# Modulation weights laid out transposed, their columns summed on VectorE

## The chip, the core and the metric

The kernel runs on one core of a Trainium2 chip. The metric is the device time of one execution in microseconds; the time before is the median of three runs. The engines are named as in the profile: PE is TensorE (matmuls and transposes) with PEld its weight loads, DVE is VectorE, ACT is ScalarE, POOL is GpSimd, SP is the queue from which all DMAs are issued. A transpose is a matmul with the identity.

## The reference, cut to what matters

A trunk of two layers works on 256 tokens of 1024 features, in float32. Each layer has three sub-layers, and each sub-layer is a norm with a modulation that depends on one conditioning vector `c`:

```python
cond = jax.nn.silu(c)
for layer in range(DEPTH):
    mod = cond @ mod_w[layer] + mod_b[layer]          # (1, 9 * 1024)
    sh1, sc1, g1, sh2, sc2, g2, sh3, sc3, g3 = jnp.split(mod, 9, axis=-1)
    h = rms_norm(x, norm_g[layer, 0]) * (1 + sc1) + sh1
    x = x + 0.5 * g1 * swiglu(h, w_gate, w_up, w_down)
    ...                                               # attention or convolution, then a second SwiGLU
return rms_norm(x, final_norm_g)
```

A SwiGLU has 2816 hidden columns. The mixer of layer 0 is a gated spatial product and an attention side by side, that of layer 1 a short convolution. `mod_w` is (2, 1024, 9216), so 18 vectors of 1024 values are each a product of `cond` with a 1024 x 1024 block of weights (4 MB); it is a matrix times a vector.

## The kernel before, in words

The residual stream is kept transposed, features on the 128 partitions and tokens along the free axis (`xT`, eight chunks of 128 features). Each float32 operand of a product is split into a part of 12 bits (`h_...`, a copy on ACT, `split_hi`) and a rest (`l_...`, a subtraction on DVE, `split_lo`), and a product is three float32r matmuls (`mm3`, line 140 in the profile, since all matmuls are recorded in the helper `mm`). Weights come in units of 1 MB by `load` (line 300) into four raw buffers (`w_g`, `w_u`, `w_d` and so on); each half of a unit is split, and a raw buffer is free when both rests are made. Helpers record all operations, so line 177 is every two-operand DVE operation, 188 every DVE operation with a scalar and a tensor, 183 every one with scalars alone, 204, 209 and 214 the activations, copies and scalings on ACT, 223 the masks on POOL.

Every engine works in the order in which the program emits. A planner (`Pace`, `clk`) keeps estimated times for each engine; `pump` and `fill_dve` issue the splits of coming weights and the steps of the modulation where they fit before the products issued so far end.

The modulation beyond the first two vectors: `mod_load` (line 390, `mw`) brings 256 rows of one block, 1 MB, rows of 4 KB. `mod_step` multiplies 128 rows x 512 columns by the matching part of `cond` (one value for each partition) and adds it to an accumulator `acc` on DVE; 16 such steps make a vector. `mod_flush` then sums over the partitions: four transposes on PE into `pm`, a row sum on DVE (`red`), and `mod_column` adds bias and gain. `mod_need` forces all of a vector before its use. There are 16 such vectors.

The start (lines 1214 to 1415) is written out by hand. `c` is transposed, `cond` made; the squares of x are summed by row, x over its rms is transposed for the norm (`pxn`) and x itself for the residual (`px`); small vectors come in five loads as rows and are transposed. Then, for each of eight chunks of 128 features (`dc`): the shift and scale columns of the chunk (`start_mod`, line 1230, `mws`, four DMAs of 256 KB with rows of 512 B) are accumulated in eight steps (`start_steps`, two on ACT and six on DVE), summed over the partitions by eight matmuls with a column of ones (`start_sum`, `pm_start`), and finished by two small DVE operations; `start_h` makes the modulated chunk `t1s` and its part `hh` on ACT, DVE the rest `hl`; then 36 products with the chunk's rows of the first three pairs of hidden columns (units `s`, 384 KB for gate and up each, rows of 3 KB) are added in the banks `ps`. After the eighth chunk the other columns of the first SwiGLU follow (`pf`), two of them ahead of the rows of its second product (`pd`). The mixer's sub-layer begins with `peh`, its scores are `z`, its spatial weights are loaded at line 870 as `ws_in` and transposed in `turn_ws` into `wsT`. The tiles `wsT`, `vb`, `qT` and `kT` serve as spare weight halves through the first SwiGLU.

Of the kernel before, what the change touches and what calls it, by code (L numbers as in the profile page):

```python
# [93 lines left out]
def trunk(ctx: ExitStack, tc: tile.TileContext, x, c, mod_w, mod_b, norm_g,  # L94
          ffn_w_gate, ffn_w_up, ffn_w_down, hy_w_in, hy_w_out, gm_vnorm_g,
          gm_w_s, gm_b_s, sc_w_in, sc_conv_w, sc_w_out, final_norm_g, out):
# [131 lines left out]
    rows_c = const.tile([8, P], F32, name="rows_c")  # L228
    nc.sync.dma_start(out=rows_c, in_=c.rearrange("b (r p) -> (b r) p", p=P))
    x_in = new(rawp, "raw", "x_in", RAW, (P, 2048)).rearrange("p (t d) -> p t d", t=2)  # L230
    for t in range(2):
        nc.sync.dma_start(out=x_in[:, t, :], in_=x[0, t * P:(t + 1) * P, :])
        clk.put(x_in[:, t, :], 6000.0 + 1600 * t)
    clk.put(rows_c, 3700.0)
    clk.dma = 5700.0
# [16 lines left out]
    # columns: norm_g (2 x 3 x 8) | final_norm_g (8) | conv_w (3 x 8) | vnorm_g (4)  # L252
    rows_a = const.tile([84, P], F32, name="rows_a")
    rows_b = const.tile([72, 2, P], F32, name="rows_b")
    cols_a = const.tile([P, 84], F32, name="cols_a")
    cols_b = const.tile([P, 2, 72], F32, name="cols_b")
    cond = const.tile([P, NC], F32, name="cond")
    G0, FG, CW, VG = 0, 48, 56, 80

    def load_rows(more):  # L260
        if not more:
            nc.sync.dma_start(out=rows_a[0:48, :], in_=norm_g.rearrange("l s (r p) -> (l s r) p", p=P))
            nc.sync.dma_start(out=rows_b, in_=mod_b.rearrange("l (r p) -> r l p", p=P))
        else:
            nc.sync.dma_start(out=rows_a[48:56, :], in_=final_norm_g.rearrange("(r p) -> r p", p=P))
            nc.sync.dma_start(out=rows_a[56:80, :], in_=sc_conv_w.rearrange("o w (r p) -> (o w r) p", p=P))
            nc.sync.dma_start(out=rows_a[80:84, :], in_=gm_vnorm_g.rearrange("o (r p) -> (o r) p", p=P))

# [116 lines left out]
    def mod_load():
        i = mq["load"]
        l, v = mod_units[i // 4]
        part = i % 4
        raw = new(mrawp, "mraw", f"mw{l}{v}{part}", MRAW, (P, 2048))
        nc.sync.dma_start(out=raw.rearrange("p (k n) -> p k n", k=2),  # L390
                          in_=mod_w[l, part * 256:(part + 1) * 256, v * D:(v + 1) * D].rearrange(
                              "(k p) n -> p k n", p=P))
# [8 lines left out]
    def can_mod():  # L401
        return mq["units"] < len(mod_units) and mq["step"] // 4 < len(mod_loaded) and \
            (mq["step"] % 16 or len(mod_pending) < 3)

    def mod_step():
        """a row chunk of the weights times its part of cond, added to one of the two halves"""
        n = mq["step"]
        l, v = mod_units[mq["units"]]
        raw, t = mod_loaded[n // 4]
        kc, h = n % 16 // 2, n % 2  # L410
        if kc == 0:
            mq["acc", h] = new(accp, "acc", f"acc{l}{v}{h}", 4, (P, 512))
# [11 lines left out]
        if kc == 7:
            mod_pending.append((l, v, h, acc, clk.dve))
            if h == 1:
                mq["units"] += 1

    def mod_column(l, v, h, src, dst):
        """adds the bias; scales become a = g * (1 + scale), the halved residual its 0.5"""  # L430
        one = slice(4 * h, 4 * h + 4)
        if v % 3 == 1:
            stt(dst, src, 1.0, mod_g(l, v)[:, one], ALU.mult, ALU.mult)
            tt(dst, dst, bias_c[:, l, v * 8 + 4 * h:v * 8 + 4 * h + 4], ALU.add)
        else:
            half = v % 3 == 2 and v // 3 != 1
            stt(dst, src, 0.5 if half else 1.0, bias_c[:, l, v * 8 + 4 * h:v * 8 + 4 * h + 4], ALU.mult, ALU.add)
# [5 lines left out]
    def mod_flush(force=False):  # L443
        """sums one unit over the partitions"""
        if not mod_pending or (mod_pending[0][4] + 200 > clk.pe and not force):
            return
        l, v, h, acc, t = mod_pending.pop(0)
# [3 lines left out]
        if (l, v) not in mod_cols:  # L451
            mod_cols[(l, v)] = const.tile([P, NC], F32, name=f"mod{l}{v}")
        dst = mod_cols[(l, v)][:, 4 * h:4 * h + 4]
        red = new(accp, "red", f"red{l}{v}{h}", 3, (P, 4))

        def finish():
            sum_v(red, pm.rearrange("p (j n) -> p j n", j=4))
            mod_column(l, v, h, red, dst)
# [1030 lines left out]
```

## Time and profile before

| | before |
|---|---|
| median of three runs | 1007.77 us (1007.18 to 1008.58) |
| span of the profiled execution | 1006.8 us |
| PE busy | 995.6 us (99%), 8176 matmuls |
| DVE busy | 790.6 us (79%), 1230 instructions |
| ACT busy | 502.9 us (50%) |
| POOL busy | 16.7 us (2%) |
| HBM read | 247.32 MB, 247 GB/s over the span |
| chain that ended last | PE 95%; SPq 2%; DMA 2% |

The chain that ended last is followed back from the last instruction, at each step to what released it. Busy time of PE overlaps between neighbouring matmuls, which are pipelined. "DMA share" is the mean busy share of the core's 16 DMA engines; it can come out a little above 1. [...]

### The profile page before, as it was taken

The page shows a single profiled execution, that of the slowest core. Times are in us where ns is not written, and L with a number is a line of the kernel's source. Part 1 is how long each engine was busy: PE and PEld are TensorE (multiplying, and loading weights), DVE is VectorE, ACT ScalarE, POOL GpSimd, SP SyncE. Part 2 cuts the span into 40 slices and gives each one's busy share as a digit, 9 for nine tenths or more (in the row PEclk, how much of TensorE's full clock was granted, in tenths as well). Part 3 has the DMA queues.
Part 4 walks back from the last instruction along what each step waited for, and adds up shares of the span by engine and source line. Part 5 has one row for each costly group of instructions (what it writes and reads, how often), then busy time and mean ns, then how long its engine had stood idle before and what let it go on. Part 6 is the DMA issues. An engine that isn't in the chain of part 4 may idle for free.

```text
span 1006.8 us, 19541 instructions
## 1 busy us (share of the span) xinstructions
PE 995.6 (99%) x8176; PEld 981.4 (97%) x8176; DVE 790.6 (79%) x1230; ACT 502.9 (50%) x716; POOL 16.7 (2%) x28
## 2 busy tenths in 40 slices
PE   7999999999999999999999999999999999999998
PEld 7899999999789999999999999999999999999998
DVE  6788978889878998878789888878899797444532
ACT  6575434355756754343367434335644465434333
POOL 0000000000320000000000000000000000000000
PEclk9999999999999999999999999999999999999999
DMA  9998987965866499887964988798359538555401
GB/s 281 323 371 296 355 318 277 328 216 177 331 236 205 132 309 358 299 313 279 323 208 157 346 302 324 273 329 280 125 171 327 172 102 281 205 194 183 168 2 42
DMA packets 159857, 249.63 MB, mean 248 GB/s; under 512 B 4525, under 2 KB 125337, under 8 KB 159769
## 3 DMA queue, kind: packets, MB, share of 16 engines
q1 hardware_dynamic: 159768, 248.39, 71.8%
q8 instruction: 64, 1.05, 0.4%
q14 instruction: 25, 0.20, 0.1%
HBM read 247.32 MB, written 1.05 MB: 247 GB/s over the span
## 4 chain that ended last, share of the span: by engine, by line
PE 95%; SPq 2%; DMA 2%; DVE 0%; ACT 0%; issue 0%; ACTq 0%
PE pf L140 43%; PE pd L140 25%; PE pe L140 3%; PE pc L140 3%; PE pdh L140 2%; PE pcb L140 2%; PE pdc L140 2%; PE ps L140 2%; PE pm L144 1%; SPq L1230 1%; PE z L140 1%; PE pu L140 1%; PE pvb L140 1%; PE peh L140 1%; PE pec L140 1%; PE pv L140 1%
## 5 line engine op out<-in xcount | busy, mean ns | idle before, releaser
L140 PE MATMUL pd<-ah,h_d 128*128 128x256 f32 x704 | 200.0, 284 | 0.0
L140 PE MATMUL pd<-ah,l_d 128*128 128x256 f32 x704 | 198.3, 282 | 0.0
L140 PE MATMUL pd<-al,h_d 128*128 128x256 f32 x704 | 197.8, 281 | 0.0
L140 PE MATMUL pf<-hh,h_u 128*128 128x256 f32 x608 | 171.8, 283 | 0.0
L140 PE MATMUL pf<-hh,l_g 128*128 128x256 f32 x608 | 171.1, 281 | 0.0
L140 PE MATMUL pf<-hh,h_g 128*128 128x256 f32 x608 | 171.0, 281 | 0.0
L140 PE MATMUL pf<-hl,h_g 128*128 128x256 f32 x608 | 171.0, 281 | 0.0
L140 PE MATMUL pf<-hl,h_u 128*128 128x256 f32 x608 | 170.9, 281 | 0.0
L140 PE MATMUL pf<-hh,l_u 128*128 128x256 f32 x608 | 170.8, 281 | 0.0
L188 DVE SCALAR_TENSOR_TENSOR acc<-mw,cond,acc 128x512 f32<-128x512 f32 x224 | 158.3, 750 | 3.1 <-DMA mw<-in_mod_w_dram 3.1
L209 ACT CAST h_d<-w_d 128x1024 fp32r<-128x1024 f32 x88 | 88.4, 1047 | 127.1 <-PE pf L140 102.5
L177 DVE TENSOR_TENSOR l_d<-w_d,h_d 128x1024 fp32r<-128x1024 f32 x88 | 104.7, 1221 | 48.2 <-ACT h_d L209 48.2
L177 DVE TENSOR_TENSOR l_g<-w_g,h_g 128x1024 fp32r<-128x1024 f32 x82 | 100.0, 1220 | 52.1 <-ACT h_g L209 52.1
L209 ACT CAST h_g<-w_g 128x1024 fp32r<-128x1024 f32 x82 | 85.8, 1047 | 108.7 <-issue 75.2
L140 PEld LDWEIGHTS pd<-al,h_d 128*128 128x128 f32 x704 | 132.7, 188 | 0.0
L140 PEld LDWEIGHTS pd<-ah,h_d 128*128 128x128 f32 x704 | 132.5, 188 | 0.0
L140 PEld LDWEIGHTS pd<-ah,l_d 128*128 128x128 f32 x704 | 132.5, 188 | 0.0
L209 ACT CAST h_u<-w_u 128x1024 fp32r<-128x1024 f32 x82 | 85.9, 1047 | 65.2 <-PE pd L140 51.2
L140 PEld LDWEIGHTS pf<-hl,h_u 128*128 128x128 f32 x608 | 114.9, 189 | 0.0
L140 PEld LDWEIGHTS pf<-hh,l_u 128*128 128x128 f32 x608 | 114.8, 189 | 0.0
L140 PEld LDWEIGHTS pf<-hh,l_g 128*128 128x128 f32 x608 | 114.8, 189 | 0.0
L140 PEld LDWEIGHTS pf<-hh,h_u 128*128 128x128 f32 x608 | 114.7, 189 | 0.0
(324 smaller groups left out, 2041.2 us busy)
## 6 DMA issues: line engine op xcount, KB each, us to landing
mw<-in_mod_w_dram SPq DMA_DIRECT2D x64, 1024.0 KB, 8.2
w_d<-in_ffn_w_down_dram SPq DMA_DIRECT2D x44, 1024.0 KB, 7.1
w_g<-in_ffn_w_gate_dram SPq DMA_DIRECT2D x41, 1024.0 KB, 7.2
w_u<-in_ffn_w_up_dram SPq DMA_DIRECT2D x41, 1024.0 KB, 5.5
mws<-in_mod_w_dram SPq DMA_DIRECT2D x28, 256.0 KB, 6.2
w_ho<-in_hy_w_out_dram SPq DMA_DIRECT2D x4, 1024.0 KB, 10.9
w_cc<-in_sc_w_in_dram SPq DMA_DIRECT2D x4, 1024.0 KB, 5.2
w_cx<-in_sc_w_in_dram SPq DMA_DIRECT2D x4, 1024.0 KB, 5.2
```

What stands on the lines that cost most here:

```text
L140: return nc.tensor.matmul(out=out_, lhsT=lhsT, rhs=rhs, start=start, stop=stop, skip_group_check=True)
L144: nc.tensor.transpose(out=out_, in_=in_, identity=idn)
L177: nc.vector.tensor_tensor(out=out_, in0=a, in1=b, op=op)
L188: nc.vector.scalar_tensor_tensor(out=out_, in0=a, scalar=s, in1=b, op0=op0, op1=op1)
L209: nc.scalar.copy(out=out_, in_=in_)
L1230: nc.sync.dma_start(out=parts[i][:, :, v, :], in_=src[:, :, v, dc * P:(dc + 1) * P])
```

## The change

The arrays are handed over in other layouts. `mod_w` becomes (layer, vector, chunk, feature on the partition, 1024 inputs): a chunk of 128 outputs is one contiguous block of 512 KB. x comes transposed, the spatial weights too, and all small vectors come as one array of columns, 128 x 228. `cond` is now wanted along the free axis on all partitions: eight small matmuls with a selector spread it to 128 x 1024. One column of 128 modulation values is one DVE operation, `dot_v`: a product of 128 x 1024 weights with `cond`, times a gain, summed along the row, with the bias as first value. Accumulators, the transposes into `pm`, row sums and `mod_column` go. In the start x needs no transposes: squares, a sum by matmuls with `mean_w`, logarithm and exponential over 128 x 256 and three Newton steps give 1 / rms on all partitions; the first chunk of x over rms is made on DVE, seven on POOL (`mul_p`). The order of the eight chunks is rewritten: scale first, then shift.

```diff
-WARM = (40, 10, 0)
+WARM = (6, 14, 24)
...
-            elif can_mod() and max(clk.dve, mod_loaded[mq["step"] // 4][1]) + 660 <= t:
+            elif can_mod() and max(clk.dve, mod_ready()) + 1200 <= t:
...
+    def dot_v(src, dst, scale, init):
+        ins = [src, cond] + aps(scale, init)
+        fill_dve(ins, [dst, src])
+        nc.vector.tensor_tensor_reduce(out=src, in0=src, in1=cond, scale=scale, scalar=init, op0=ALU.mult,
+                                       op1=ALU.add, accum_out=dst)
+        return clk.op("dve", free(src) / 0.96 + 130, ins, [dst, src])
...
+    def mul_p(out_, a, b):
+        nc.gpsimd.tensor_tensor(out=out_, in0=a, in1=b, op=ALU.mult)
...
+    xT = const.tile([P, NC, S], F32, name="xT")
+    for i in range(2):
+        nc.sync.dma_start(out=xT[:, 4 * i:4 * i + 4, :], in_=x[:, 4 * i:4 * i + 4, :])
+    cols_sb = const.tile([P, 228], F32, name="cols_sb")
+    nc.sync.dma_start(out=cols_sb, in_=cols)
...
     def mod_load():
-        raw = new(mrawp, "mraw", f"mw{l}{v}{part}", MRAW, (P, 2048))
-        nc.sync.dma_start(out=raw.rearrange("p (k n) -> p k n", k=2),
-                          in_=mod_w[l, part * 256:(part + 1) * 256, v * D:(v + 1) * D].rearrange(
-                              "(k p) n -> p k n", p=P))
+        raw = new(mrawp, "mraw", f"mw{l}{v}{part}", MRAW, (P, 2, D))
+        nc.sync.dma_start(out=raw, in_=mod_w[l, v, 2 * part:2 * part + 2].rearrange("c p k -> p c k"))
...
     def mod_step():
-        if kc == 0:
-            ts(acc, src, cond[:, 0:1], None, ALU.mult)
-        else:
-            stt(acc, src, cond[:, kc:kc + 1], acc, ALU.mult, ALU.add)
+        dot_v(mod_loaded[n // 2][0][:, n % 2, :], mod_cols[(l, v)][:, chunk:chunk + 1], scale,
+              cols_b[:, l, v * 8 + chunk:v * 8 + chunk + 1])
...
-    def mod_flush(force=False):
-        pm = gbank(f"pm{l}{v}{h}")
-        for j in range(4):
-            tp(pm[:, j * P:(j + 1) * P], acc[:, j * P:(j + 1) * P], ident)
...
-            nc.sync.dma_start(out=ws_in[k], in_=gm_w_s[0, 4 * k:4 * k + 4].rearrange("h t s -> t h s"))
+        wsT = new(mix, "wsT", "wsT", 1, (P, 8, P))
+        nc.sync.dma_start(out=wsT, in_=gm_w_s)
+        keep_if(wsT, [[0, 8], [1, P]], ALU.is_ge)
...
-        def turn_ws(k):
-            for j in range(4):
-                tp(pw[:, j * P:(j + 1) * P], ws_in[k][:, j, :], ident)
...
     def start_mod(dc):
-            for v in range(2):
-                nc.sync.dma_start(out=parts[i][:, :, v, :], in_=src[:, :, v, dc * P:(dc + 1) * P])
+        for v in (1, 0):
+            nc.sync.dma_start(out=parts[v], in_=mod_w[0, v, dc])
...
+    sel = new(hip, "hi", "sel", HALF, (P, 1024), F32R).bitcast(F32)[0:8].rearrange("p (r m) -> p r m", r=8)
+    copy_v(sel, ident[0:8, 0:8].unsqueeze(2).to_broadcast([8, 8, P]))
+    for i in range(8):
+        mm(pcs[i // 4][:, i % 4 * P:(i % 4 + 1) * P], sel[:, i, :], ce, i % 4 == 0, True)
+    for k in range(2):
+        act(sqs[0][:, k], xT[:, 2 * k:2 * k + 2, :], AF.Square)
+    copy_v(cond[:, 0:512], pcs[0])
+    tt(sqs[0][:, 0], sqs[0][:, 0], sqs[0][:, 1], ALU.add)
+    for k in range(2):
+        act(sqs[1][:, k], xT[:, 4 + 2 * k:6 + 2 * k, :], AF.Square)
+    cp(cond[:, 512:D], pcs[1])
+    tt(sqs[1][:, 0], sqs[1][:, 0], sqs[1][:, 1], ALU.add)
+    for i in range(2):
+        for j in range(2):
+            mm(pr, mean_w, sqs[i][:, 0, j, :], i == j == 0, i == j == 1)
+    act(y0, pr, AF.Ln, bias=eps_t[:, 0:1])
+    act(y0, y0, AF.Exp, scale=-0.5)
+    newton(pr, y0, r0, m0, EPS)
+    for dc in range(NC):
+        o = xnT[dc // 4][:, dc % 4, :]
+        if dc < 1:
+            tt(o, xT[:, dc, :], r0, ALU.mult)
+        else:
+            mul_p(o, xT[:, dc, :], r0)
...
+    start_col(0, 1)
+    start_col(0, 0)
+    split_hi()
+    split_lo()
     for dc in range(NC):
+        t1 = start_h(dc)
+        if dc == 0:
+            split_hi()
         if dc + 3 < NC:
             mws[dc + 3] = start_mod(dc + 3)
         while can_load() and q["load"] < min(dc + 3, NC):
             load()
         tt(hl[:, dc, 0:S], t1, hh[:, dc, 0:S].bitcast(F32), ALU.subtract)
+        if dc + 1 < NC:
+            start_col(dc + 1, 1)
+        if dc == NC - 1:
+            while can_load():
+                load()
+        split_lo()
+        for i in range(2):
+            split_hi()
+        if dc + 1 < NC:
+            start_col(dc + 1, 0)
+        split_lo()
         parts = [take() for _ in range(2)]
-        for f in range(2 * NS):
-            if dc < NC - 1 and f == SUMS[dc]:
-                start_sum(dc + 1)
+        for i in range(2):
+            j, wh, wl = parts[i]
+            for f in range(2 * NS):
```

`start_col(dc, v)` is `dot_v` on the scale (`v` = 1) or shift (`v` = 0) of a chunk; `start_h` is now only the two ACT operations. The calls of `mod_flush` and `turn_ws` go.

## Rows read from the trace of the kernel before

**Rows 1.** Windows: us, busy us of each engine, granted clock, DMA share, GB/s.

```profile
215.00:345.00 130.00, 130.00 (x952) 118.63 (x951) 114.35 (x204) 83.19 (x135) 15.22 (x18) 1.00 0.62 215
64.43:996.60 932.17, 932.17 (x7698) 920.65 (x7698) 739.81 (x1104) 458.72 (x638) 15.22 (x18) 1.00 0.71 245
```

**Rows 2.** Chain of waits, end of the start: start us, us, what.

```profile
55.65 8.78 PE ps L140 x72
```

**Rows 3.** Timeline of the start: start us, us, engine, instruction [idle before].

```profile
4.68 1.06 ACT L204 ACTIVATE sqx<-x_in 128x1024 f32<-128x1024 f32 x1 [1.91 <-DMA x_in<-in_x_dram]
5.64 0.18 ACT L204 ACTIVATION_READ_ACCUMULATOR sqx<-x_in 128x1 f32 x1
...
14.70 0.40 ACT L209 CAST hh<-t1s 128x256 fp32r<-128x256 f32 x1
...
15.14 0.42 DVE L177 TENSOR_TENSOR hl<-t1s,hh 128x256 fp32r<-128x256 f32 x1 [0.30 <-ACT hh L209]
...
15.16 0.39 PE L140 MATMUL ps<-hh,h_s 128*128 128x256 f32 x1
```

**Rows 4.** Windows of the start and of a stretch after it, columns as above.

```profile
16.00:52.00 36.00, 32.36 (x244) 30.61 (x244) 28.00 (x67) 20.82 (x37) 0.00 (x0) 0.95 1.07 318
33.00:36.00 3.00, 3.00 (x14) 3.00 (x15) 2.43 (x7) 2.35 (x4) 0.00 (x0) 0.50 1.16 293
66.00:72.00 6.00, 6.00 (x53) 6.00 (x52) 4.94 (x9) 5.22 (x10) 0.00 (x0) 1.00 1.03 410
```

**Rows 5.** DMA issues: count, KB each, median us to landing.

```profile
mws<-in_mod_w_dram SPq DMA_DIRECT2D x28, 256.0 KB, 6.2
...
w_s<-in_ffn_w_gate_dram SPq DMA_DIRECT2D x8, 384.0 KB, 5.9
```

**Rows 6.** Tile `w_s`: idle time of its engine, us and times, until:

```profile
  DMA w_s<-in_ffn_w_gate_dram: 7.1, 4
```

**Rows 7.** Chain of waits, first SwiGLU's end and attention.

```profile
206.46 0.44 PE pm L144 x4
206.90 14.24 PE pd L140 x120
...
275.83 0.59 PE pm L144 x4
```

**Rows 8.** Groups on VectorE, whole span: busy us, mean ns, idle before.

```profile
L188 DVE SCALAR_TENSOR_TENSOR acc<-mw,cond,acc 128x512 f32<-128x512 f32 x224 | 158.3, 750 | 3.1 <-DMA mw<-in_mod_w_dram 3.1
L177 DVE TENSOR_TENSOR l_d<-w_d,h_d 128x1024 fp32r<-128x1024 f32 x88 | 104.7, 1221 | 48.2 <-ACT h_d L209 48.2
...
L177 DVE TENSOR_TENSOR al<-act,ah 128x512 fp32r<-128x512 f32 x44 | 30.4, 691 | 16.9 <-ACT ah L209 16.5
...
L198 DVE TENSOR_REDUCE red<-pm 128x4 f32<-128x512 f32 x32 | 21.9, 686 | 8.1 <-PE pm L144 8.1
```

**Rows 9.** Timeline of VectorE at the end of the start.

```profile
57.68 0.43 DVE L177 TENSOR_TENSOR hl<-t1s,hh 128x256 fp32r<-128x256 f32 x1 [1.11 <-ACT hh L209]
58.03 1.82 DVE L177 TENSOR_TENSOR l_s<-w_s,h_s 128x768 fp32r<-128x768 f32 x2
...
61.28 1.23 DVE L177 TENSOR_TENSOR l_u<-w_u,h_u 128x1024 fp32r<-128x1024 f32 x1
62.42 1.22 DVE L177 TENSOR_TENSOR l_g<-w_g,h_g 128x1024 fp32r<-128x1024 f32 x1
```

**Rows 10.** Groups on ScalarE, whole span.

```profile
L204 ACT ACTIVATE sq<-xT 128x512 f32<-128x512 f32 x20 | 12.7, 633 | 19.3 <-DVE xT L188 15.6 <-DVE sqacc L177 3.7
...
L204 ACT ACTIVATE y_pe<-pr_pe,eps_t 128x256 f32<-128x256 f32 x3 | 1.4, 478 | 5.7 <-PE pr_pe L140 5.7
```

**Rows 11.** Timeline of SP in the mixer.

```profile
243.16 1.12 SPq L870 DMA_DIRECT2D ws_in<-in_gm_w_s_dram  x2
```

**Rows 12.** Groups on GpSimd, whole span.

```profile
L223 POOL TENSOR_SCALAR_AFFINE_SELECT sp<-sp 128x256 f32<-128x256 f32 x8 | 6.9, 864 | 279.6 <-DVE sp L188 279.6
...
L223 POOL TENSOR_SCALAR_AFFINE_SELECT wsT<-wsT 128x512 f32<-128x512 f32 x2 | 2.7, 1350 | 0.0
```

More of the change, by code (lines that the diff above doesn't have):

```diff
@@ L229, in trunk @@
     nc.sync.dma_start(out=rows_c, in_=c.rearrange("b (r p) -> (b r) p", p=P))
[L230 to L235, printed above, removed]
+    xT = const.tile([P, NC, S], F32, name="xT")
+    for i in range(2):
+        nc.sync.dma_start(out=xT[:, 4 * i:4 * i + 4, :], in_=x[:, 4 * i:4 * i + 4, :])
+        clk.put(xT[:, 4 * i:4 * i + 4, :], 3600.0 + 1300 * i)
+    G0, FG, CW, VG, MB = 0, 48, 56, 80, 84
+    cols_sb = const.tile([P, 228], F32, name="cols_sb")
+    nc.sync.dma_start(out=cols_sb, in_=cols)
+    clk.put(cols_sb, 5500.0)
+    cols_a = cols_sb[:, 0:MB]
+    cols_b = cols_sb[:, MB:MB + 144].rearrange("p (l r) -> p l r", l=2)
+    clk.put(rows_c, 2300.0)
+    clk.dma = 5500.0
     ident = const.tile([P, P], F32, name="ident")
@@ L249, in trunk @@
     keep_if(negtri, [[-1, P]], ALU.is_ge, 1)
[L253 to L263, printed above, removed]
[L264 to L267 removed]
+    cond = const.tile([P, D], F32, name="cond")
     units = []
@@ L307, in can_load @@
         u = q["load"]
-        return u < len(units) and (u < RAW - 1 or ("x" if u == RAW - 1 else u - RAW) in raw_free)
+        return u < len(units) and (u < RAW or u - RAW in raw_free)
     slots = {}
@@ L401, in can_mod, with mod_ready @@
     def can_mod():
-        return mq["units"] < len(mod_units) and mq["step"] // 4 < len(mod_loaded) and \
-            (mq["step"] % 16 or len(mod_pending) < 3)
+        return mq["step"] // 2 < len(mod_loaded)
+    def mod_ready():
+        return mod_loaded[mq["step"] // 2][1]
     def mod_step():
         n = mq["step"]
-        l, v = mod_units[mq["units"]]
-        raw, t = mod_loaded[n // 4]
-        kc, h = n % 16 // 2, n % 2
-        if kc == 0:
-            mq["acc", h] = new(accp, "acc", f"acc{l}{v}{h}", 4, (P, 512))
-        acc, src = mq["acc", h], raw[:, (n % 4) * 512:(n % 4 + 1) * 512]
-        if kc == 0:
-            ts(acc, src, cond[:, 0:1], None, ALU.mult)
-        else:
-            stt(acc, src, cond[:, kc:kc + 1], acc, ALU.mult, ALU.add)
+        l, v = mod_units[n // 8]
+        chunk = n % 8
+        if chunk == 0:
+            mod_cols[(l, v)] = const.tile([P, NC], F32, name=f"mod{l}{v}")
+        scale = 1.0
+        if v % 3 == 1:
+            scale = mod_g(l, v)[:, chunk:chunk + 1]
+        elif v % 3 == 2 and v // 3 != 1:
+            scale = 0.5
+        dot_v(mod_loaded[n // 2][0][:, n % 2, :], mod_cols[(l, v)][:, chunk:chunk + 1], scale,
+              cols_b[:, l, v * 8 + chunk:v * 8 + chunk + 1])
         mq["step"] += 1
-        if n % 4 == 3:
-            mraw_free[n // 4] = clk.dve
-            mod_loaded[n // 4] = None
+        if n % 2 == 1:
+            mraw_free[n // 2] = clk.dve
+            mod_loaded[n // 2] = (None, 0.0)
             while can_mod_load():
                 mod_load()
[L424 to L437, printed above, removed]
     def mod_g(l, v):
@@ L441, in mod_g @@
         return cols_a[:, g:g + 8]
[L443 to L471 removed]
+    def mod_need(l, v):
+        while mq["step"] < 8 * (mod_units.index((l, v)) + 1):
+            mod_step()
     deferred = []
@@ L1259, in trunk @@
     clk.op("dve", 120.0, [ce], [ce])
-    tt(cond, pc[:, 0:8], ce, ALU.mult)
-    ss = const.tile([P, 2], F32, name="ss")
-    sy = const.tile([P, 2], F32, name="sy")
-    sr = const.tile([P, 2], F32, name="sr")
-    sqx = new(hip, "hi", "sqx", HALF, (P, 1024), F32R).bitcast(F32)
-    xn = [new(lop, "lo", f"xn{t}", HALF, (P, 1024), F32R).bitcast(F32) for t in range(2)]
-    for t in range(2):
-        act(sqx, x_in[:, t, :], AF.Square, accum_out=ss[:, t:t + 1])
-        clk.put(ss[:, t:t + 1], clk.act)
-        one = slice(t, t + 1)
-        ts(ss[:, one], ss[:, one], 1.0 / D, EPS, ALU.mult, ALU.add)
-        act(sy[:, one], ss[:, one], AF.Ln)
-        act(sy[:, one], sy[:, one], AF.Exp, scale=-0.5)
-        newton(ss[:, one], sy[:, one], sr[:, one], ss[:, one])
-        ts(xn[t], x_in[:, t, :], sr[:, one], None, ALU.mult)
@@ L1332, in trunk @@
-    accs = {}
-    def start_h(dc):
-        one = slice(dc, dc + 1)
-        stt(m_a[:, one], pm0[:, 2 * dc + 1:2 * dc + 2], cols_a[:, G0 + dc:G0 + dc + 1], cols_b[:, 0, 8 + dc:9 + dc], ALU.mult, ALU.add)
-        tt(m_sh[:, one], pm0[:, 2 * dc:2 * dc + 1], cols_b[:, 0, one], ALU.add)
-        t1 = new(work, "t1", f"t1s{dc}", 4)
-        act(t1, xnT[dc // 4][:, dc % 4, :], AF.Identity, scale=m_a[:, one], bias=m_sh[:, one])
-        cp(hh[:, dc, 0:S], t1)
-        return t1
-    start_steps(0, range(NC))
@@ L1360, in prepare, with start_col, start_h @@
             ts(bv[:, sub, 2], bv[:, sub, 2], 0.5, None, ALU.mult)
+    newton(pr, y0, r0, m0, EPS)
+    xnT = [mix.tile([P, 4, S], F32, tag=tag, name="xn" + tag) for tag in ("qT", "kT")]
     for dc in range(NC):
-        def steps(ks):
-            start_steps(dc + 1, ks)
-        def hs():
-            while q["h"] < 2 * dc + 2:
-                split_hi()
-        if dc > 1:
-            steps(range(2))
-        hs()
-        if dc == 1:
-            x_copies.pop()()
-            raw_free["x"] = clk.act
+        o = xnT[dc // 4][:, dc % 4, :]
[3 more added lines that the diff above has]
+            mul_p(o, xT[:, dc, :], r0)
+    hh = new(mix, "hh", "hh00", 1, (P, NC, XC), F32R)
+    hl = new(mix, "hl", "hl00", 1, (P, NC, XC), F32R)
+    state["h"] = (hh, hl)
+    m_sh = const.tile([P, NC], F32, name="mod00")
+    m_a = const.tile([P, NC], F32, name="mod01")
+    mod_cols[(0, 0)], mod_cols[(0, 1)] = m_sh, m_a
+    def start_col(dc, v):
+        one = slice(dc, dc + 1)
+        if v:
+            dot_v(mws[dc][1], m_a[:, one], cols_a[:, G0 + dc:G0 + dc + 1], cols_b[:, 0, 8 + dc:9 + dc])
+        else:
+            dot_v(mws[dc][0], m_sh[:, one], 1.0, cols_b[:, 0, one])
+    def start_h(dc):
+        one = slice(dc, dc + 1)
+        t1 = new(work, "t1", f"t1s{dc}", 4)
+        act(t1, xnT[dc // 4][:, dc % 4, :], AF.Identity, scale=m_a[:, one], bias=m_sh[:, one])
+        cp(hh[:, dc, 0:S], t1)
+        return t1
+    start_col(0, 1)
+    start_col(0, 0)
+    split_hi()
+    split_lo()
+    sbanks = [gbank(f"ps{f}") if f < 4 else dbank(f"ps{f}") for f in range(2 * NS)]
+    for dc in range(NC):
+        t1 = start_h(dc)
+        if dc == 0:
+            split_hi()
         if dc + 3 < NC:
```

175 lines of the change are left out of this document (38 added, 137 removed).

## The prediction

> **What bounds the kernel now.** I read the windows by stage first. From 64.43 to 996.60 us TensorE is busy 932.17 of 932.17 us at a granted clock of 1.00, while VectorE is at 739.81 and the DMA share at 0.71 [rows 1]. There a microsecond of TensorE work that disappears is a microsecond of time, and work on VectorE costs nothing until it delays an operand of a product. The start is another kernel: its products `ps` run from 15.16 to 64.43 us [rows 2, 3]. Inside it the DMA share is 1.07 and yet only 318 GB/s move, while 410 GB/s move a little later at a share of 1.03 [rows 4]; the later stretch fetches rows of 4 KB, the start mostly rows of 512 B. The casts of the weights, which stand on ScalarE in front of each chunk's `hh`, wait 7.1 us for weights [rows 6].
>
> **The change, part by part.** The sum is made against the profiled span of 1006.8 us; the median of the runs, 1007.77 us, lies 0.97 us above it, which I carry over.
>
> *Transposes of the modulation sums.* The 128 transposes of `pm` go (16 vectors, two halves, four each). On the chain of waits a group of four takes 0.44 us, a few in the attention 0.59 [rows 7]. 32 x 0.44 = 14.1 us, at most 32 x 0.59 = 18.9. They stand among products that wait for nothing, so 14.1 us go from the end. The eight transposes of the spatial weights are two groups of the same kind: 0.9 us. In the attention such groups may fill gaps of a dependent chain; eight of them stand there, some 3.5 us to 4.7, which a gap could take back. TensorE shows no idle time from 215 to 345 us [rows 1], so I count them as gained and keep their loss for the range.
>
> *VectorE, steady part.* Out go 224 updates (158.3 us) and 32 row sums (21.9) [rows 8], together 180 us, and 32 first steps and the small columns besides. In come 128 `dot_v`, each a product of two 1024-wide float32 operands with a sum beside it. The trace has no such operation. From below: the plain 1024-wide TENSOR_TENSOR, 1.22 us long and followed after 1.14 us [rows 9]. From above: two cycles for each element. The 1024-wide and the 512-wide TENSOR_TENSOR (1221 and 691 ns) differ by 0.53 us for 512 elements [rows 8], so 1024 elements more in cycles add 1.06: 2.2 us. Nearest is the plain row, plus 0.06 us for scalars read by pointer (750 against 691 ns for 512 elements), plus something for delivering the sum, where ScalarE's accumulator read shows 0.18 us [rows 3]. I take 1.28 us from one start to the next. 128 x 1.28 = 164 us against 180: VectorE gets lighter, off the path, and the time stays.
>
> *The start, head.* Out go 32 transposes of x, three of small vectors, their copies on ScalarE and 64 matmuls of column sums. In come four squares (0.63 us each), a logarithm and an exponential of 256 columns (0.48 each) [rows 10], three Newton steps on VectorE, four matmuls. x's first half is there at 4.68 us, as now [rows 3]; its second at 5.9, as half a megabyte at 0.4 MB/us takes 1.3. Squares end at 7.1, their sum on VectorE at 7.8 (0.69, as the 512-wide row), four float32 matmuls at some 8.8 (estimate), logarithm and exponential at 9.8, Newton and the first chunk of x over rms (four steps of 0.4, by `hl`) at 11.5, two dots at 14.1, then the modulated chunk on ScalarE (0.6, an addressed scale and bias) and `hh` (0.40): the first product starts at about 15.1, as now [rows 3]. Removing the transposes of x gains nothing at the head; it moves the wait from TensorE to the line of norm and dots.
>
> *The start, cadence.* Eight chunks of 128 features follow one another. TensorE needs 36 products each; 72 take 8.78 us [rows 2], so 4.4. The DMA brings 1.05 MB of modulation and 0.79 MB of weights [rows 5]: 5.8 us at the present 318 GB/s, 4.6 at 400. Each modulation row is now 4 KB instead of 512 B and each weight row stays at 3 KB, so I take 400. VectorE has `hl` 0.35, two splits 1.82 [rows 9], two dots 2.56 and some 0.25 us of waiting for `hh` behind the second dot: 4.97 us. VectorE binds. Now the eight `hl` run from 15.14 to 57.68 us [rows 3, 9], 6.08 us apart. New: 15.1 + 7 x 4.97 + 4.7 = 54.6 us for the end of `ps`, against 64.43: a gain of 9.8 us. All chunks (15.9 MB with x) have landed at 43 us by that rate; the next two loads of 1 MB wait only for buffers that VectorE's rests free, and land before 54.
>
> *Queues.* On SP 32 loads of modulation become 16, and five loads of small vectors become one ahead of them; nothing there is late. The spatial weights now go straight into `wsT`, which holds spare weight halves until the first SwiGLU's products end at 221.1 us [rows 7]; the present loads are issued at 243.16 [rows 11]. So no wait on SP, where `bs_bc` and the next weights are queued behind. The mask on GpSimd is one pass of 1024 columns for two of 512 (1.35 us each) [rows 12], earlier than now, on an idle engine; without that cover it would cost 2.7 us once. Seven products of x over rms go to GpSimd, one needed per chunk; its row with 256 columns takes 0.86 us [rows 12], so they end about 6 us after Newton and stay ahead of a chunk each 4.97.
>
> Sum: 14.1 + 0.9 + 9.8 = 24.8 us. 1006.8 - 24.8 + 0.97 = **983 us**.
>
> **Rivals.**
>
> *The dots run at half rate (slower).* Price 2.2 us each. In the start VectorE's cadence becomes 0.35 + 1.82 + 4.4 + 0.25 = 6.8 us, the first product comes at 17, `ps` ends at 17 + 7 x 6.8 + 4.7 = 69.3: 4.9 us lost. In the steady part 282 us of dots replace some 202, so VectorE stands at 820 of 917 us; and the order of issue is written by a planner whose formula counts 1.2 us a dot, so each dot keeps splits and SwiGLU products waiting a microsecond longer than planned. Of these 128 us VectorE's idle time, 192 us [rows 1], takes most; I put a fifth, 24 us, on TensorE: 1007.8 + 4.9 - 15.0 + 24 = 1022. It is slower from 11 us of such stalls upward. Against it: an update with two SBUF operands takes 750 ns for 512 elements [rows 8], the full rate. [...] Chance 0.08.
>
> *The start stays bound by the DMA, or its head is late.* If 318 GB/s are not a matter of row length, the cadence is 5.8 us and `ps` ends at 15.1 + 7 x 5.8 + 4.7 = 60.4, a gain of 4.0 instead of 9.8: **989 us**. The same time comes out if GpSimd's seven products (6 us) hold up VectorE's first dots. [...] Against: 410 GB/s in rows 4. [...] Chance 0.22, with the case that the attention takes back its 3.5 us (986).
>
> *The start gains more.* With dots at 1.14 and no wait for `hh` the DMA's 4.6 binds: 15.1 + 7 x 4.6 + 4.7 = 52.0, so 980. That is the forecast's own lower side.
>
> *The removed transposes do not show.* They are on the chain, so only if TensorE's place is taken by something not seen: 0.02.
>
> **How the numbers follow.** Forecast (980 to 986) 0.68, DMA or head (986 to 995) 0.22, half rate 0.08, nothing 0.02. The range goes from 977, where the `pm` groups in the attention count 0.59 and the head comes 2 us earlier, to 994, the second rival with the attention's loss; it leaves out the half-rate case and little else. About 0.2% (2 us) is what a measurement of this kernel can tell from no change. Faster 0.90, same 0.02, slower 0.08.
>
> **What would show it.** Right: no rows of `pm` and `pws`; a dot followed after about 1.28 us; TensorE without idle time from the end of `ps`, which lies at 54 to 55 us; eight `hl` 5.0 us apart; over 370 GB/s in the start. Wrong: dots above 2 us, TensorE idle between the end of `ps` and 790 us; or casts that wait for weights through the start at 320 GB/s.

## The result, and the profile after

The changed kernel takes 990.77 us (median of four runs, 990.55 to 990.80) against 1007.47 us (median of four, 1006.60 to 1008.58) for the kernel before in the same comparison: ratio 0.9835, 95% interval 0.9822 to 0.9848. That is faster, as forecast, and 7.8 us above the forecast of 983. The profiled execution has a span of 989.1 us and a time of its own of 990.8 us, so 1.7 us lie around the span where the prediction carried 0.97: 0.7 us of the miss. In the later runs of the kernel before, too, the time is 1.7 to 1.8 us above the span of the same run, so the execution that I had profiled, with 1006.8 us, was about 0.8 us longer than the median one. The other 7.1 us are in the trace, and one view finds them: the chain of waits at the end of the start.

```profile
56.70 0.41 ACT hh L216
...
57.13 0.44 DVE hl L176
...
57.62 4.53 PE ps L139 x35
62.14 7.98 PE pf L139 x67
```

The start ends at 62.14 us (before 64.43): 2.3 us gained where 9.8 were forecast. From there to the end are 926.96 us (before 942.4): 15.4 us gained where 15.0 were forecast. So the steady part came out as predicted, well within the 2 us by which runs of the kernel before differ, and the start misses 7.5 us.

**Steady part.** Windows of the changed kernel (us, busy us of PE, PEld, DVE, ACT, POOL, granted clock as a share of full speed, DMA share, GB/s), which answer to [rows 1]:

```profile
215.00:345.00 130.00, 129.90 (x950) 118.81 (x949) 113.04 (x198) 85.27 (x138) 13.35 (x17) 1.00 0.60 215
...
62.14:979.00 916.86, 916.76 (x7559) 905.51 (x7558) 709.72 (x1029) 457.57 (x635) 13.35 (x17) 1.00 0.71 249
```

TensorE is still the bound: 916.76 busy of 916.86 us. Groups on VectorE (busy us, mean ns, idle before):

```profile
L199 DVE CUSTOM_DVE_ANT_0 mw<-mw,cond,cols_sb 128x1024 f32<-128x1024 f32 x128 | 163.7, 1306 | 3.4 <-DMA mw<-in_mod_w_dram 3.4
...
L199 DVE DVE_READ_ACCUMULATOR2_ANT mod<- 128x1 f32 x144 | 11.7, 81 | 0.0
```

A dot of 1024 columns takes 1306 ns and a read of the accumulator of 81 ns that lies beside the next instruction. 128 of them are 164 us; `acc` and `red` [rows 8] took 180.

**Start.** VectorE's timeline of the changed kernel (start us, us, instruction, idle before):

```profile
8.04 0.69 DVE L176 TENSOR_TENSOR sqx<-sqx 128x512 f32<-128x512 f32 x1 [0.46 <-ACT sqx L211]
...
14.20 0.42 DVE L187 SCALAR_TENSOR_TENSOR m_start<-pr_start,y_start 128x256 f32<-128x256 f32 x1 [5.39 <-ACT y_start L211]
...
15.92 1.74 DVE L199 CUSTOM_DVE_ANT_0 mws<-mws,cond,cols_sb 128x1024 f32<-128x1024 f32 x1
...
17.60 1.73 DVE L199 CUSTOM_DVE_ANT_0 mws<-mws,cond,cols_sb 128x1024 f32<-128x1024 f32 x1
...
19.26 1.47 DVE L176 TENSOR_TENSOR l_s<-w_s,h_s 128x768 fp32r<-128x768 f32 x1
20.65 0.94 DVE L176 TENSOR_TENSOR hl<-t1s,hh 128x256 fp32r<-128x256 f32 x1
...
26.28 0.95 DVE L176 TENSOR_TENSOR l_s<-w_s,h_s 128x768 fp32r<-128x768 f32 x1
27.53 0.42 DVE L176 TENSOR_TENSOR hl<-t1s,hh 128x256 fp32r<-128x256 f32 x1 [0.30 <-ACT hh L216]
27.87 1.34 DVE L199 CUSTOM_DVE_ANT_0 mws2vb<-mws2vb,cond,cols_sb 128x1024 f32<-128x1024 f32 x1
...
57.13 0.43 DVE L176 TENSOR_TENSOR hl<-t1s,hh 128x256 fp32r<-128x256 f32 x1
```

Three things are to be seen. Newton's first step starts at 14.20 us after a wait of 5.39 us; the forecast had it at 9.8. The first `hl` comes at 20.65 (before 15.14 [rows 3]) and the second 6.88 us later, not 4.97. From the second to the eighth the distance is (57.13 - 27.53) / 6 = 4.93 us, as forecast. And until about 25 us the same shapes are slow: dots 1.74 us against 1.34, `l_s` 1.47 against 0.95, `hl` 0.94 against 0.42. GpSimd's timeline covers just that stretch:

```profile
15.63 4.28 POOL L229 TENSOR_TENSOR xnqT<-xT,r_start 128x256 f32<-128x256 f32 x3 [13.14 <-DVE r_start L187]
19.88 5.39 POOL L229 TENSOR_TENSOR xnkT<-xT,r_start 128x256 f32<-128x256 f32 x4
```

The wait ahead of Newton is explained by the chain of waits of the head:

```profile
2.88 0.95 DVE ce L1198
...
4.19 3.77 PE pt_c L139 x16
7.96 3.18 PE pt_warm L143 x14
11.14 2.08 PE pr_start L139 x8
...
13.25 0.48 ACT y_start L211
```

The squares are summed at 8.73 us (8.04 + 0.69), but `pr_start` stands behind 14 warming transposes and starts at 11.14. (The eight float32 matmuls of the spread stand there as x16, so x8 are the four column sums.) The 8.73 are themselves late, by 0.9 us: the second half of x is squared from 6.86 us on, where the forecast had it at 5.9. Rows of ScalarE and TensorE:

```profile
6.86 1.15 ACT L211 ACTIVATE sqx<-xT 128x512 f32<-128x512 f32 x2 [0.41 <-DMA xT<-in_x_dram]
...
20.46 0.58 PE L139 MATMUL ps<-hh,h_s 128*128 128x256 f32 x1 [4.63 <-ACT hh L216]
```

TensorE's granted clock reads 0.75 and 0.50 around the gap between the warming transposes and the first product:

```profile
17.00:20.00 3.00, 0.00 (x0) 0.00 (x0) 3.00 (x5) 0.60 (x1) 3.00 (x3) 0.75 1.03 423
20.00:23.00 3.00, 1.93 (x7) 1.64 (x8) 3.00 (x3) 2.61 (x4) 3.00 (x3) 0.50 1.02 415
```

### The profile page after: what moved, and what is told of

Read it like the earlier page. It is cut to its first block, busy times and chain, and to the rows that moved or that the text cites. A ratio compares the mean times of both kernels' runs of the same rounds, so it can differ in the third digit from the quotient of the medians.

```text
span 989.1 us, 18921 instructions
## 1 busy us (share of the span) xinstructions
PE 975.3 (99%) x7958; PEld 959.7 (97%) x7958; DVE 764.0 (77%) x1118; ACT 491.8 (50%) x691; POOL 24.7 (3%) x34
## 3 DMA queue, kind: packets, MB, share of 16 engines
q8 instruction: 62, 1.02, 0.4%
## 4 chain that ended last, share of the span: by engine, by line
PE 94%; DVE 4%; ACT 1%; DMA 1%; issue 0%; DVEq 0%; SPq 0%; ACTq 0%
PE pf L139 44%; PE pd L139 25%; PE pc L139 3%; PE pe L139 3%; PE pcb L139 2%; PE pdc L139 2%; DVE mws L199 1%; PE pdh L139 1%; PE z L139 1%; PE pu L139 1%; PE pvb L139 1%; PE peh L139 1%; PE pec L139 1%; PE pv L139 1%; PE ps L139 1%; PE py L139 1%
## 5 line engine op out<-in xcount | busy, mean ns | idle before, releaser
L139 PE MATMUL pd<-ah,h_d 128*128 128x256 f32 x704 | 198.0, 281 | 0.0
L199 DVE CUSTOM_DVE_ANT_0 mw<-mw,cond,cols_sb 128x1024 f32<-128x1024 f32 x128 | 163.7, 1306 | 3.4 <-DMA mw<-in_mod_w_dram 3.4
L139 PEld LDWEIGHTS pf<-hh,h_g 128*128 128x128 f32 x608 | 114.8, 189 | 0.0
```

The lines of the kernel that those rows point to most:

```text
L139: return nc.tensor.matmul(out=out_, lhsT=lhsT, rhs=rhs, start=start, stop=stop, skip_group_check=True)
L199: nc.vector.tensor_tensor_reduce(out=src, in0=src, in1=cond, scale=scale, scalar=init, op0=ALU.mult, op1=ALU.add, accum_out=dst)
```

## The experiments

My theory after the comparison: the steady part is the transposes; the start lost its gain to a head written in series (norm, then dots), to warming transposes in front of the sums, and to GpSimd's products beside VectorE's. The rivals were that the steady gain had another source, that the slow stretch came from the transfers, and that the start hides behind them. Below, a ratio is to the kernel before in the same comparison, as above, and a span with a sign is the change against the changed kernel's 989.1 us. e1, e5, e6 and e11 are one execution each; the other times are medians of four, in e12 of five. The changed kernel's own runs lie within 0.25 us.

**e1: put the transposes back.**

```diff
+    def flush(force=False):
...
+            pm = gbank("pm")
+            for j in range(4):
+                tp(pm[:, j * P:(j + 1) * P], ident, ident)
```

> The changed kernel with its 128 modulation transposes put back as 32 groups of four (of the identity, into a bank that nobody reads), at the places where the kernel before had them; the sums stay on VectorE. My theory: after the start TensorE sets the time, so each group costs what its row of before showed, 0.44 us: +14.1 us, 1004.9 us. Rival one: gaps of the attention take eight groups back, +10.6 us, 1001.4. Rival two: the 15.4 us that the steady part gained come from lighter VectorE work and fewer waits for banks, not from the transposes themselves: under +6 us, below 997.

Measured 1004.35 us, span 1002.6: +13.5 us on the span. Two pieces of its chain of waits, in the first SwiGLU and in the attention:

```profile
204.08 0.44 PE pm L143 x4
...
273.02 0.59 PE pm L143 x4
```

So 13.5 of the steady part's 15.4 us are the transposes, 0.42 us a group. Of the 14.1 expected only 0.6 us are missing, so the attention takes little back, and both rivals fall. The remaining 1.9 us hold the spatial weights' two groups (0.9 us by the forecast) and about 1 us that I don't assign; the longer than usual execution of the kernel before, 0.8 us, would nearly fill it.

**e2: the dots of chunk 0 ahead of the Newton steps.**

```diff
+    start_col(0, 1)
+    start_col(0, 0)
     newton(pr, y0, r0, m0, EPS)
...
-    start_col(0, 1)
-    start_col(0, 0)
     split_hi()
```

> The two dots of chunk 0 are emitted ahead of the Newton steps instead of behind x over rms; nothing else moves. My theory: the head is late because norm and dots stand one behind the other on VectorE, which waits for 5.39 us in front of the Newton steps with all inputs of the dots there. The dots go into that wait, the first hl comes at about 17.2 us instead of 20.65, and the end of ps moves with it: -3 to -3.5 us, about 987.5. Rival one: the head hides behind transfers (weights or modulation of the next chunks): under -1 us. Rival two: chunk 0 gains, but the products on GpSimd now slow chunk 1's dots and splits by as much as they slowed chunk 0's, and half is lost: -1.5 us.

Measured 988.52 us, ratio 0.9804 (0.9787 to 0.9820), span -2.6. VectorE's timeline:

```profile
8.87 1.34 DVE L199 CUSTOM_DVE_ANT_0 mws<-mws,cond,cols_sb 128x1024 f32<-128x1024 f32 x1 [0.22 <-DMA mws<-in_mod_w_dram]
...
17.30 0.95 DVE L176 TENSOR_TENSOR hl<-t1s,hh 128x256 fp32r<-128x256 f32 x1
...
24.33 0.95 DVE L176 TENSOR_TENSOR hl<-t1s,hh 128x256 fp32r<-128x256 f32 x1
```

`hl` moves by 3.35 us as expected. In the end 2.65 remain: the products on GpSimd now reach into chunk 1 as far as its `hl` (0.95 us where it was 0.42), a weak form of rival two.

**e3: no warming transposes ahead of the sums.**

```diff
-WARM = (6, 14, 24)
+WARM = (6, 0, 24)
```

> The 14 warming transposes ahead of the column sums of the squares are taken out (6, 0 and 24 instead of 6, 14 and 24). My theory: pr_start waits for them, not for its squares, whose last sum ends at 8.73 us; it starts at 8.8 instead of 11.14 and all behind it moves by 2.3 us: about 988.5. [...]

Measured 989.39 us, ratio 0.9810 (0.9795 to 0.9824), span -1.4. TensorE's timeline:

```profile
7.95 3.78 PE L139 MATMUL pr_start<-sqx,mean_w 128*128 128x256 f32 x8
```

The sums start 3 us earlier and end only 1.5 us earlier: they take 3.78 us instead of 2.28 (10.93 to 13.21 in the same view of the changed kernel). The theory was right on when the sums start and left out their pace. A record of the sums lasts 634 ns here and 379 ns at the end of the changed kernel's. The granted clock reads 1.00 in these stretches all the same, so I tell this pace by the length of records alone.

**e4: x over rms on VectorE, none on GpSimd.**

```diff
-            mul_p(o, xT[:, dc, :], r0)
...
         if dc + 1 < NC:
+            tt(xn[dc + 1], xT[:, dc + 1, :], r0, ALU.mult)
             start_col(dc + 1, 0)
```

> The seven products of x over rms leave GpSimd: VectorE makes each just ahead of its chunk's second dot. My theory: VectorE's instructions with two operands are slowed by GpSimd's products beside them. Without them a dot in the head takes 1.34 us instead of 1.74, a split 0.95 instead of 1.48, hl 0.42 instead of 0.94; that gives 3.4 us, and VectorE pays 7 x 0.36 = 2.5 us in its cadence, which goes to some 5.3 us: together -0.9 us, 989.9. Rival: the slow stretch has another cause (transfers at over 400 GB/s into the same memory at the same time): dots stay near 1.74 us and the time is 2.5 us longer, 993.3.

Measured 990.51 us, ratio 0.9821 (0.9807 to 0.9836), span -0.7, the end of `ps` at 61.13 us (-1.0). By its interval the ratio can't be told from the changed kernel's 0.9835; the verdict rests on VectorE's timeline:

```profile
15.97 1.34 DVE L199 CUSTOM_DVE_ANT_0 mws<-mws,cond,cols_sb 128x1024 f32<-128x1024 f32 x1
...
17.23 1.28 DVE L199 CUSTOM_DVE_ANT_0 mws<-mws,cond,cols_sb 128x1024 f32<-128x1024 f32 x1
...
18.44 0.96 DVE L176 TENSOR_TENSOR l_s<-w_s,h_s 128x768 fp32r<-128x768 f32 x1
19.63 0.43 DVE L176 TENSOR_TENSOR hl<-t1s,hh 128x256 fp32r<-128x256 f32 x1 [0.23 <-ACT hh L216]
```

The transfers run as in the changed kernel (421 GB/s from 17 to 20 us) and the slow durations are gone: it was GpSimd. Beside its products a dot takes 1.74 us instead of 1.34, a split of 768 columns 1.47 instead of 0.96 and an `hl` 0.94 instead of 0.43, so the cost is 30 to 120 per cent. VectorE's own price is 0.28 us a chunk, 2.0 in all, against 3.0 gained in the head and the first chunks.

**e5: the start's modulation weights in pieces of 512 B.**

```diff
-            nc.sync.dma_start(out=parts[v], in_=mod_w[0, v, dc])
+            nc.sync.dma_start(out=parts[v].rearrange("p (a k) -> p a k", a=8),
+                              in_=mod_w[0, v, dc].rearrange("p k -> (p k)").rearrange(
+                                  "(a p k) -> p a k", a=8, k=P))
```

> The sixteen loads of modulation weights in the start are read in pieces of 512 B, as before the change, instead of rows of 4 KB; the weights then stand in another order, so the first sub-layer's modulation vectors (and the output) are other numbers. It asks whether the faster cadence of the start needed the new layout or only the dots. My theory: with 512 B pieces the queues move about 320 GB/s as before, 1.84 MB per chunk take 5.75 us, more than VectorE's 4.93, casts on ScalarE wait for weights again, the eight hl stand 5.7 us apart later in the start and the time is 4 to 5 us longer, about 995. Rival: the transfers run ahead far enough, or are as fast as now; hl stay 4.93 us apart, 990.8.

Measured 990.97 us, span 989.2: nothing. `hl` stands at 27.66, 32.60, 37.54, 42.48 and so on, 4.94 us apart. My theory fell. While the queues are full the pieces do matter (347 GB/s from 17 to 20 us, against 423), but with VectorE setting the pace and a late head the transfers have time to spare, and no cast waits for weights in either. In the kernel before, the start did wait for the transfers. Three pieces of its chain of waits, an issue of `mws` on SP and two transfers of `w_s`:

```profile
16.19 3.28 SPq L1230
...
22.25 5.50 DMA w_s<-in_ffn_w_gate_dram
...
34.30 7.02 DMA w_s<-in_ffn_w_up_dram
```

But from 20 to 40 us 317 GB/s moved there, and 362 with the 512 B pieces of e5. What made that difference stays open.

**e6: longer dots in the steady part.**

```diff
+        src = mod_loaded[n // 2][0][:, n % 2, 0:768]
+        nc.vector.tensor_tensor(out=src, in0=src, in1=cond[:, 0:768], op=ALU.mult)
```

> Behind each of the 128 dots of the steady part stands one more VectorE product of 768 columns (0.95 us, 0.89 from start to start), of which the planner knows nothing; nobody reads it. A dot then costs about the 2.2 us of the rival with half rate, 114 us more VectorE work in all. By my forecast's pricing of that rival a fifth of it reaches TensorE: +18 to +24 us, 1009 to 1015. Rival one: VectorE's idle time takes all: under +3 us. Rival two: VectorE becomes the bound in some stage and more than half arrives, over +60 us.

Measured 1016.0 us, span 1014.3: +25.2 us of the 114 added, 22 per cent. Waits of TensorE in this run (us in total, times, longest):

```profile
PE pe L139 <- ACT hh L221: 5.8, 2, 3.3
...
PE peh L139 <- ACT hh L221: 4.6, 1, 4.6
...
PE pec L139 <- ACT hh L221: 4.0, 1, 4.0
```

These are the entries of sub-layers, where all dots of the next scale are forced before the operands are made: 14.4 us. The rest I can't place fully; TensorE's busy time also grew by 9.6 us, and the granted clock stands at 0.96 from 215 to 345 us. VectorE off the path is not free here: 22 per cent arrive, near the fifth that the rival's price had put without a working.

**e7: the gap ahead of the spread of cond filled, four transposes ahead of the sums.**

```diff
-WARM = (6, 14, 24)
+WARM = (11, 4, 24)
```

> Warming transposes 11, 4 and 24 instead of 6, 14 and 24: they fill the gap of 1.23 us ahead of the spread of cond, and only four stand ahead of the column sums. My theory: without the 14 the column sums start at about 8.7 us, but where they were taken away alone the sums ran at 0.63 us a record instead of 0.38; with TensorE busy without a gap from 1.4 us on, the fast pace should begin earlier: sums end at 10.4 to 10.8 instead of 13.22, and the start is 2.4 to 2.8 us shorter, about 988.2. Rival: the pace does not depend on that gap; the sums run at 0.63 and end near 12.3: -0.9 us, about 989.9.

Measured 990.04 us, ratio 0.9827 (0.9811 to 0.9844), span -0.7, again not to be told from the changed kernel by the ratio alone. The trace decides for the rival: the sums run at 634 ns and end at 12.5 us.

**e8: e2, e4 and e7 together**, with 34 transposes behind the sums.

> All three at once: chunk 0's dots ahead of the Newton steps, x over rms on VectorE chunk by chunk, warming transposes 11, 4 and 34. My theory, from the parts: column sums end at 10.5 us, Newton from 11.5, hl of chunk 0 at about 14.4 instead of 20.65, then 5.2 us per chunk (4.93 and the product): the end of ps at 14.4 + 7 x 5.2 + 4.9 = 55.7 instead of 62.14, -6.4 us, about 984.4. Rival: the weights and modulation of the first chunks are not there that early and the transfers bind the first chunks: half of it, about 987.5.

Measured 986.82 us, ratio 0.9796 (0.9781 to 0.9810), span -4.3. `hl` of chunk 0 at 16.33 us instead of 14.4, since the sums run slow here too (634 ns a record); from there 5.21 us per chunk, as expected. The 34 transposes fill TensorE's gap and the granted clock is 1.00 throughout. It fell short by the slow sums, not by the transfers.

**e9: 17 transposes ahead of the spread of cond.**

```diff
-WARM = (6, 14, 24)
+WARM = (17, 11, 24)
```

> Warming transposes 17, 11 and 24 instead of 6, 14 and 24. In the kernel before, transposes fell from 0.42 to 0.27 us a record after some 3.2 us of nothing but transposes; in the changed kernel and the runs on its warming they did so 3.3 to 4.2 us after the spread of cond had ended, whether or not its gap was filled. [...] Then 17 transposes ahead of it bring the pace at 4.7 us, the spread takes about half of its 3.8 us and ends near 7.3, the column sums run at 0.38 from 8.7 on and end near 10.7 instead of 13.22: -2.4 us, about 988.3. Rival: the pace has nothing to do with what is done, or is lost again during the spread; then cond is 1 us later and the sums end near 12.5 or later: -0.7 to +0.5 us.

Measured 987.72 us, ratio 0.9810 (0.9785 to 0.9835), span -3.1. TensorE's timeline:

```profile
1.42 3.60 PE L143 MATMUL pt_warm<-ident 128*128 128x128 f32 x17 [1.42 <-POOL ident masks.py:199]
4.96 2.05 PE L139 MATMUL pt_c<-ce,sel 8*128 8x128 f32 x16
6.94 1.42 PE L143 MATMUL pt_warm<-ident 128*128 128x128 f32 x11
8.19 1.89 PE L139 MATMUL pr_start<-sqx,mean_w 128*128 128x256 f32 x8
```

The fast pace comes within the 17 (421 ns a record from 3 to 4 us, 297 from 4.7 us on), the spread takes 2.05 us instead of 3.77, and the sums end at 10.1 instead of 13.2. One of its four runs lay at 992.31, 4.6 us above the others and above the changed kernel; it has no trace. e12 takes that up.

**e10: everything ahead.** e2, 17/11/34 transposes, and the products of e4 one chunk earlier, in the place where VectorE waited for `hh`.

```diff
         split_lo()
+        if dc + 2 < NC:
+            tt(xn[dc + 2], xT[:, dc + 2, :], r0, ALU.mult)
...
```

> Chunk 0's dots ahead of the Newton steps, warming transposes 17, 11 and 34, and x over rms on VectorE, but each chunk's product one chunk earlier, behind the second split, where VectorE waits 0.24 us for hh. My theory: hl of chunk 0 at 14.4 us, then 0.34 + 1.74 + 0.34 + 2.51 = 4.93 to 5.0 us per chunk, the end of ps at 14.4 + 7 x 5.0 + 4.9 = 54.3 instead of 62.14, -7.8 us, about 983. Rival: the pace of TensorE in the head stays as it was and hl comes at 16.3; then the end of ps lies at 56.2, -5.9 us, about 985.

Measured 984.34 us, ratio 0.9765 (0.9749 to 0.9782), span 982.0, the end of `ps` at 55.45 us. VectorE's timeline:

```profile
14.40 0.42 DVE L176 TENSOR_TENSOR hl<-t1s,hh 128x256 fp32r<-128x256 f32 x1
...
19.28 0.42 DVE L176 TENSOR_TENSOR hl<-t1s,hh 128x256 fp32r<-128x256 f32 x1
...
24.16 0.96 DVE L176 TENSOR_TENSOR l_s<-w_s,h_s 128x768 fp32r<-128x768 f32 x1 [1.13 <-ACT h_s L216]
```

The first `hl` is where it was expected and the chunks are 4.88 us apart, but one: in chunk 2 ScalarE's cast waits 4.06 us for weights and VectorE behind it 1.7. With VectorE out of the way the transfers (402 GB/s from 16 to 46 us, at a share of 1.02) begin to bind.

**e11: the same with pieces of 512 B.** The edit is that of e5.

> The arrangement with everything ahead (dots of chunk 0 first, products of x over rms one chunk early on VectorE, warming 17, 11 and 34), but the modulation weights of the start read in pieces of 512 B; the first sub-layer's modulation vectors and the output are then other numbers. In the changed kernel the 512 B pieces cost nothing, since VectorE and the late head set the pace. Here casts on ScalarE wait for weights (8.2 us in all) with 4 KB rows already. My theory: pieces of 512 B move some 360 GB/s instead of 415 while the queues are full, 13 per cent less; the third to seventh chunk then arrive later by up to 4 us, VectorE waits for casts, and the end of ps comes 2 to 5 us later than 55.45, the time 986 to 989. Rival: the lead of the transfers over VectorE still covers it, under +1 us.

Measured 986.98 us, the end of `ps` at 58.23 us: 2.8 us later, as expected, but for another reason. `hl` of chunk 0 came at 18.62 us because the spread ran slow again, with the same 17 transposes in front:

```profile
5.24 3.78 PE L139 MATMUL pt_c<-ce,sel 8*128 8x128 f32 x16
```

From there the chunks are 4.88 us apart, with one slip of 0.4. What the pieces would cost behind a fast head this run can't tell.

**e12: a margin for the pace.** e10 with 24, 5 and 34 transposes.

> As the arrangement with everything ahead, with warming transposes 24, 5 and 34 instead of 17, 11 and 34. With 17 ahead of the spread of cond the pace of TensorE rose at 4.3 to 4.5 us, just within the 17, in two profiles; in the look with 512 B pieces it did not rise within them, spread and column sums ran slow, and hl of chunk 0 came at 18.6 us. My theory: the 17 are too few by a hair, not the 512 B pieces at fault; 24 leave room, the spread starts some 0.6 us later at the fast pace, the column sums end near 10.6 us, the end of ps comes at 55.5 to 56.3 and all runs lie within 1 us of each other: about 984.5. Rival: the rise is a matter of chance whatever stands ahead; some runs lie 3 to 5 us above the others.

Measured 983.90 us (983.59 to 984.27, five runs), ratio 0.9765 (0.9752 to 0.9778), span 981.8, the end of `ps` at 55.38 us. TensorE's timeline:

```profile
1.42 5.38 PE L143 MATMUL pt_warm<-ident 128*128 128x128 f32 x24 [1.42 <-POOL ident masks.py:199]
6.73 2.18 PE L139 MATMUL pt_c<-ce,sel 8*128 8x128 f32 x16
8.84 0.77 PE L143 MATMUL pt_warm<-ident 128*128 128x128 f32 x5
9.49 1.97 PE L139 MATMUL pr_start<-sqx,mean_w 128*128 128x256 f32 x8
```

All five runs lie within 0.7 us. `hl` of chunk 0 is 1.2 us later than in e10 (15.56), which the transfers absorb: the end of the start is the same. This version beats both kernels. That the 24 leave room is not shown, though. TensorE's groups in this run from 6.0 to 6.5 and from 7 to 8 us:

```profile
L143 PE MATMUL pt_warm<-ident 128*128 128x128 f32 x4 | 1.1, 418 | 0.0
...
L139 PE MATMUL pt_c<-ce,sel 8*128 8x128 f32 x10 | 1.5, 294 | 0.0
```

All 24 transposes run slow, and the records shorten only in the spread behind them, near 7 us, where in e9 and e10 they did so near 4.5. So the moment moves by over 2 us between executions, and the 24 were just enough in this one. With 17 in front, e11's execution ran slow and, by its time, one of e9's four, but none of e10's four. Five even runs with 24 don't exclude the rival, chance.

## Why the prediction was right and wrong

- **Transposes, 15.0 us: right.** 15.4 came, and e1 gives 13.5 of them back with the transposes alone.
- **Dots at 1.28 us, VectorE lighter in the steady part: right.** 1306 ns a dot, and the next instruction starts 1.26 or 1.21 us after it where GpSimd is quiet (e4's timeline), a little sooner than forecast. The rival of half rate is excluded by the row: 1024 elements in 1.31 us with the sum delivered is close to the plain row's 1.22 [rows 9]. Its 2.2 us rested on an assumed two cycles for each element, which no run shows. The rival's price, a fifth of the added work, was a guess that e6 bears out.
- **Cadence of 4.97 us: right in size** (4.93) and in what binds, VectorE. The 400 GB/s on which it was said to depend were not needed, as e5 shows. That the length of the pieces alone bound the start before is therefore not shown; the transfers did bind it up to 41.3 us (the chain shown at e5), at a rate that e5's pieces don't reproduce. The expected sign, over 370 GB/s in the start, was wrong too: 335 from 16 to 52 us, at a share of 0.92, because the demand is lower.
- **Head, "the first product starts at about 15.1, as now": this step failed.** It came at 20.46 us, 5.4 late. 4.4 of them have come together by "four float32 matmuls at some 8.8 (estimate)", which end at 13.22. 2.4 are the wait from 8.73 to 11.14: I took the start of the sums from their inputs and left out the order on TensorE, where the diff's `WARM` line puts 14 transposes ahead of them, behind the spread. 1.1 are the sums' own length, 2.08 us instead of the estimate's 1.0, which no run shows. 0.9 is the second half of x, which came later than "at 5.9". e9 takes 3.1 us of the 4.4 back. The dots cost 0.8 us more than 2.6 and the rest 0.1. That norm and dots stand in series was in my sum and not questioned: e2 gains 2.6 us by moving the dots into the wait.
- **GpSimd's products "stay ahead of a chunk": right, and beside the point.** They were on time, though 1.35 to 1.43 us each instead of 0.86, and slowed VectorE. I had priced it as a rival (up to 6 us) instead of a term: in the second interval 0.52 for `hl`, 0.41 and 0.47 for the dots and 0.53 for a split make the 1.9 us by which it exceeds 4.97, and with the first chunk's dots and split it is about 3.3 us.
- **The granted clock** stood at 0.50 from 20 to 23 us (before, from 33 to 36 [rows 4]). That added nothing that I can find: VectorE's delays fill the interval by themselves.

The 7.5 us add up from `hl`: the first is 5.5 us late against the 15.1 from which the forecast counts, the second interval 1.9 too long, the other six together 0.2 shorter, and from the eighth to the end of `ps` it is 0.3 more than 4.7.

So the time, 990.77 us, lies where the second rival had it (986 to 995, chance 0.22) and not in the forecast's own 980 to 986, but only in part for that rival's reasons. Of its mechanisms, GpSimd's products beside VectorE were at work; the transfers' rate did not bind. The larger part, the column sums behind the warming transposes and at the slow pace, stood in no rival. That the rival's 989 comes so near is luck. With the head mended and the products on VectorE (e12) `ps` ends at 55.4 us; the forecast had 54.6.

## What to carry to other kernels

A chain at the head of a kernel is costed engine by engine in the order of issue: write down what stands ahead of each instruction on its engine, warming work included, not only when its inputs are there. Here work moved to GpSimd was paid for by VectorE: about 0.45 us for each dot, split and `hl` beside GpSimd's products (a dot 1.74 us instead of 1.34). Count such a price as a term, and compare it with doing the work on VectorE. And put what needs only early data into the waits of the chain that needs late data.

## What was not expected of the hardware

- TensorE's pace in the head: in the kernel before a transpose record falls from 421 to 273 ns in mid-stream, between 5 and 6 us, while the granted clock reads 1.00 on both sides. In the changed kernel the records shorten near 11.5 us (634 to 379 ns), behind the spread and all 14 transposes, within the column sums; with 17 transposes ahead of the spread at about 4.5 us in e9 and e10, and in e11, with the same instructions in front, only in the last of the column sums, near 14.4 us. With 24 (e12) they did so near 7 us, behind the last of them. What moves it stays open.
- VectorE's dots, splits and `hl` lose 0.4 to 0.5 us each beside GpSimd's products, at 256 columns (0.94 us instead of 0.42) as at 768 (1.47 instead of 0.95) and 1024 (1.74 instead of 1.34).
- A reciprocal of 8 x 128 values takes 0.95 us on VectorE (`ce`, L1198) and stands on the chain of the head.
